# A hybrid decoder step on one core: a sample product over 128 rows, sample states one chunk later, and the last group's square sums read from PSUM and held back

## The chip, the cores and the metric

The kernel runs on one NeuronCore of a Trainium2 chip. The metric is the device time of one execution in microseconds. Five engines work beside each other, each with its own queue that it takes in order: TensorE (PE, matmuls and transposes into the accumulator memory PSUM), VectorE (DVE), ScalarE (ACT), GpSimd (POOL) and SyncE (SP, which issues nearly all DMAs). They wait for each other through semaphores.

## The reference

One layer of a hybrid decoder, run for a prompt of 1024 tokens with 16 learned meta tokens ahead of it, and for 8 samples of 8 tokens each with their own states. Everything is float32. Per layer:

```python
proj = rmsnorm(h, norm_mix_pre) @ w_in            # 1024 -> 4112: gate_b, gate_c, hv, z, xbc, dt
u = gate_c * hv                                   # short convolution mixer
ya = group_rmsnorm(gate_b * causal_dwconv(u, buf_sc, sconv_w), sconv_norm, 8)
xbc = silu(causal_dwconv(xbc, buf_xbc, ssm_conv_w) + ssm_conv_b)
y, s = ssd_chunked(x, softplus(dt + dt_bias), -exp(A_log), B, C, s0, chunk)   # chunks of 128
yb = group_rmsnorm((y + D_skip * x) * silu(z), ssm_norm, 2)
h = h + rmsnorm(concat(ya, yb) @ w_out, norm_mix_post)
fn = rmsnorm(h, norm_ffn_pre)
h = h + rmsnorm((silu(fn @ w_gate) * (fn @ w_up)) @ w_down, norm_ffn_post)
```

Outputs are the layer's result for prompt and samples, and the last states of both convolutions and of the recurrence. Two parts matter here. In `ssd_chunked` a sample's new state is `decay * s0 + sum over its 8 tokens of B_t (dt_t x_t)`, and its output has a term `C_t s0`. And each row of 1024 is normalised twice between the two halves of the layer: once as the out-projection's result, once as the input of the FFN.

## The kernel before

Tokens stand in ten tiles: tile 0 the 16 meta tokens, tiles 1 to 8 the prompt's chunks, tile 9 the 64 sample tokens. Products are made to float32 accuracy by splitting an operand into a rounded high half and the low rest (names in h and l) and running three products: high by high, high by low, low by high.

The program has five stages. Up to about 190 us the inputs are normalised and transposed and the xbc part of the input projection runs (px). From 190 to about 545 us is the mixing stage: for each chunk i the recurrence (`ssd_chunk`: mask tiles M built from the running decay, which is fetched from DRAM as d_a and scaled at L553; products px, po, pd, st), while the remaining parts of the input projection (pz, pc, ph, pb at L220) fill PE in between. Each projected bank in PSUM is freed by a DVE operation: for pz that is L627, for pb L662. The samples' work lies between the chunks: `samples_begin` once, then `sample_state(u)` for the eight states u (a group g of 8 heads, half of the samples, half of the group's heads). A table says after which chunk each is written:

```python
SAMP = {1: (0,), 2: (1,), 3: (2, 3), 4: (4, 5), 5: (6,), 6: (7,)}
```

A state is fetched (s0), transposed on PE into PSUM (s0p, L750), split into three bfloat16 parts (s0t, ACT at L752 and L754, DVE at L753 and L755), and used for the output term (so, L773). The new part is made by PE (s1p, L760 and L761): the samples' x rows stand as high halves in rows 0 to 63 of xs2 and low halves in rows 64 to 127. The first product takes all 128 rows against b1, the high half of B twice; the second takes rows 0 to 63 alone against b2, the low half of B. B is masked per sample into b1 and b2 (bm, L740). DVE scales the old state (L764), adds the new part (L766), and the sum goes to DRAM. s0p, s1p, px and st share two double banks of PSUM (`big`).

From about 528 to 684 us the out-projection runs in three groups of tiles, (1,2,3), (4,9,5), (6,7,8): weights wo are split on ACT (woh, L998) and DVE (wol, L999), and multiplied with the mixed rows' high halves mhb (ACT, L954) and low halves mlb (DVE, L98) into the accumulators o (L1009). Its first group starts while the short convolution's last norms are still made: square (ACT), group sums sn (PE, L668), root (ACT, L669), reciprocal (DVE, L672).

Then the FFN. `residual` takes h = x + rmsnorm(o): a square sum on ACT (ms, L147), the factor on DVE and POOL (mr), and two DVE operations (L899, L900). `fn_tile` makes the FFN's input: square sum (hs), factor (hr), hn (DVE, L916), transposes fT on PE. The FFN's up-projection uses a seven-product scheme of Strassen's kind on blocks of tokens and weights (from 742 to 1163 us; first products from 686); its blocks B01, B11, T1 to T4, B22 are sums of blocks of hn, split at L1191. `first(q)` runs the product whose tokens are ready first: xg and xu over B01, a copy of each accumulator aside (p1g, p1u, ACT at L1079), then on over B11. The copies must be done before PE may go on into the same accumulator. The down-projection follows to the end.

What is written in Python is not the order of the queues: a scheduler walks the program with a simulated timeline and orders each engine's instructions by readiness and by the priorities in `tc.high_priority(offset=...)`. So an edit in one place can reorder the queues far from it.

## Time and profile before

| | |
|---|---|
| Times of three runs | 1406.12, 1403.69, 1406.01 us (median 1406.01) |
| The profiled execution | 1402.11 us, span 1400.4 us |
| TensorE busy | 1369.7 us, 8841 matmul records |
| VectorE busy | 973.9 us |
| ScalarE busy | 586.2 us |
| Sample products over 128 rows (L760) | 16, from 240.9 to 449.8 us |
| Sample products over 64 rows (L761) | 16, from 241.2 to 450.2 us |

A row of a timeline gives start, duration, engine, source line, operation, output and inputs by name, shape and count; in brackets stands the idle time before it and what ended it. Matmul records overlap, so the pace of PE is the distance of starts, not the duration.

### The profile page before, as it was taken

How to read it: one execution, taken by the hardware profiler on the slowest of the kernel's cores; microseconds unless marked ns; L12 is line 12 of the kernel's file. 1: busy time of each engine (PE TensorE's matmuls, PEld its weight loads, DVE VectorE, ACT ScalarE, POOL GpSimd, SP SyncE). 2: the span in 40 equal slices, each digit the busy share in tenths (PEclk: the TensorE clock that was granted, in tenths of full speed). 3: DMA queues.
4: the chain of work that ended last, by engine and by line, in shares of the span. 5: the costliest groups of instructions: out<-in, count | busy, mean ns of one | idle time of the engine just before them, and what ended most of it. 6: DMA issues, size and time to landing. Idle time of an engine off the chain costs nothing.

```text
span 1400.4 us, 22011 instructions
## 1 busy us (share of the span) xinstructions
PE 1369.7 (98%) x8841; PEld 1230.6 (88%) x8841; DVE 973.9 (70%) x1334; ACT 586.2 (42%) x947; POOL 51.8 (4%) x106
## 2 busy tenths in 40 slices
PE   7999999999999999999899999999999999999997
PEld 5889998878888988887799999999999998888886
DVE  6654457868888988767689877666767666455565
ACT  6465345434354354656553232222332334344431
POOL 1000000000000200011100000000000000000001
PEclk9999999999999999999999999999999999999999
DMA  6135346667746457765435553444433479655554
GB/s 214 47 109 148 95 125 198 202 178 205 218 117 208 123 185 256 237 226 196 154 119 167 203 207 113 149 167 168 145 136 103 159 226 341 208 180 165 170 165 139
DMA packets 212543, 240.51 MB, mean 172 GB/s; under 512 B 33421, under 2 KB 161505, under 8 KB 212442
## 3 DMA queue, kind: packets, MB, share of 16 engines
q1 hardware_dynamic: 212442, 239.12, 53.5%
q8 instruction: 69, 1.13, 0.3%
q14 instruction: 32, 0.26, 0.1%
HBM read 170.29 MB, written 68.79 MB: 171 GB/s over the span
## 4 chain that ended last, share of the span: by engine, by line
PE 90%; DVE 3%; DMA 3%; ACT 2%; issue 1%; SPq 1%; POOL 0%; DVEq 0%; POOLq 0%; ACTq 0%
PE d L1393 15%; PE px L220 10%; PE o L1009 9%; PE yu L1050 7%; PE yg L1050 7%; PE pz L220 5%; PE zu L1050 5%; PE zg L1050 5%; PE xg L1050 5%; PE xu L1050 5%; PE pb L220 3%; PE pc L220 3%; PE ph L220 2%; DMA M<-d_a 1%; PE pd L572 1%
## 5 line engine op out<-in xcount | busy, mean ns | idle before, releaser
L220 PE MATMUL px<-xh,whi 128*128 128x272 f32 (+2 forms) x288 | 94.6, 336 | 0.1
L220 PE MATMUL px<-xl,whi 128*128 128x272 f32 (+2 forms) x288 | 93.7, 333 | 0.0
L220 PE MATMUL px<-xh,wlo 128*128 128x272 f32 (+2 forms) x288 | 93.3, 332 | 0.0
L98 DVE TENSOR_TENSOR wlo<-raw,whi 128x1024 fp32r<-128x1024 f32 x32 | 39.0, 1220 | 45.5 <-ACT whi L106 45.4
L999 DVE SCALAR_TENSOR_TENSOR wol<-wo,vec,woh 128x1024 fp32r<-128x1024 f32 x36 | 46.0, 1278 | 32.2 <-ACT woh L998 32.1
L220 PE MATMUL pz<-xh,whi 128*128 128x256 f32 (+2 forms) x192 | 64.6, 337 | 0.0
L220 PE MATMUL pz<-xh,wlo 128*128 128x256 f32 (+2 forms) x192 | 63.9, 333 | 0.0
L220 PE MATMUL pz<-xl,whi 128*128 128x256 f32 (+2 forms) x192 | 63.7, 332 | 0.0
L998 ACT ACTIVATE woh<-wo,vec 128x1024 fp32r<-128x1024 f32 x36 | 41.4, 1149 | 49.1 <-PE o L1009 45.9
L220 PEld LDWEIGHTS px<-xh,whi 128*128 128x128 f32 x288 | 54.4, 192 | 4.6 <-ACT xr L279 0.3
L220 PEld LDWEIGHTS px<-xl,whi 128*128 128x128 f32 x288 | 53.9, 190 | 4.2 <-issue 0.2
L220 PEld LDWEIGHTS px<-xh,wlo 128*128 128x128 f32 x288 | 54.0, 190 | 3.7
L1393 PE MATMUL d<-wd,B01h 128*128 128x512 f32 x176 | 54.2, 389 | 0.0
L252 DVE SCALAR_TENSOR_TENSOR xa<-xr,vec,xa 128x1128 f32<-128x1128 f32 x36 | 50.1, 1391 | 1.2 <-ACT xa L249 0.5
L1393 PE MATMUL d<-wd,T3h 128*128 128x512 f32 x152 | 46.8, 389 | 0.0
L1009 PE MATMUL o<-wol,mhb 128*128 128x512 f32 x144 | 44.4, 394 | 0.2 <-DVE wol L999 0.2
L1393 PE MATMUL d<-wd,B11h 128*128 128x512 f32 x144 | 44.1, 389 | 0.0
L1393 PE MATMUL d<-wd,T2h 128*128 128x512 f32 x144 | 44.1, 389 | 0.0
L279 ACT ACTIVATE xr<-px 128x272 f32<-128x272 f32 (+2 forms) x36 | 16.3, 456 | 60.4 <-PE px L220 60.3
L556 ACT ACTIVATE M<-M,a_tok 128x128 f32<-128x128 f32 (+1 forms) x72 | 21.7, 382 | 46.0 <-DMA M<-d_a 45.1
L1009 PE MATMUL o<-woh,mlb 128*128 128x512 f32 x128 | 40.3, 392 | 0.0
L220 PEld LDWEIGHTS pz<-xh,whi 128*128 128x128 f32 x192 | 36.1, 188 | 3.9 <-issue 1.3
(691 smaller groups left out, 4101.3 us busy)
## 6 DMA issues: line engine op xcount, KB each, us to landing
wo<-in_w_out_dram SPq DMA_DIRECT2D x36, 512.0 KB, 4.8
raw<-in_w_in_dram SPq DMA_DIRECT2D x32, 512.0 KB, 5.3
wg<-in_w_gate_dram SPq DMA_DIRECT2D x11, 1024.0 KB, 8.5
wu<-in_w_up_dram SPq DMA_DIRECT2D x11, 1024.0 KB, 5.3
xr<-in_w_down_dram SPq DMA_DIRECT2D x11, 1024.0 KB, 5.6
d_t<-xr SPq DMA_DIRECT2D x11, 1024.0 KB
xt<-in_x_prompt_dram SPq DMA_DIRECT2D x16, 512.0 KB, 4.8
M<-d_a SPq DMA_DIRECT2D x16, 512.0 KB, 5.4
```

The costliest lines, as they stand in the source:

```text
L98: V.tensor_tensor(out=out, in0=a, in1=hi.bitcast(F32), op=ALU.subtract)
L220: PE.matmul(acc, (hi, lo, hi)[q][:, wk], (xh, xh, xl)[q][t][:, k, o:], start=n_ == 0, stop=n_ + 1 == len(order))
L252: V.scalar_tensor_tensor(out=dst, in0=part(row, i), scalar=wv[:, wcol(i):wcol(i) + 1], in1=dst, op0=ALU.mult, op1=ALU.add)
L279: S.activation(row[:, rc], pt[:, pc], AF.Copy)
L556: S.activation(M[:w, h, :w], M[:w, h, :w], AF.Relu, scale=-1.0, bias=a_s)
L572: PE.matmul(pdv[64 * e:64 * e + 64, h // 2, :w], xd[:w, h * 64:(h + 1) * 64], Ms[h // 8][:w, h % 8, :w], start=True, stop=True)
L998: S.activation(hi, raw, AF.Copy, scale=nv)
L999: V.scalar_tensor_tensor(out=lo, in0=raw, scalar=nv, in1=hi[:, :].bitcast(F32), op0=ALU.mult, op1=ALU.subtract)
L1009: PE.matmul(accs[i][c], l[:, kb, :], r_[:, c * 512:(c + 1) * 512], start=n == 0 and q == 0, stop=n == 11 and q == len(steps) - 1)
L1050: PE.matmul(acc[:, c, 0:W1], w_[l][k], b[r_][:, k, c * W1:(c + 1) * W1], start=start and k == 0 and x == 0, stop=k == 3 and x == 2, skip_g ...
L1393: PE.matmul(accs[t], sx[x][:, tl], wx[y], start=st and x + y == 0, stop=en and x == 1, skip_group_check=n not in OPENS)
```

## The change

Four edits. (1) `SAMP` writes states 3, 5, 6 and 7 one chunk later. (2) The second sample product takes all 128 rows: b2 becomes one buffer of 128 rows, whose lower half is filled with zeros once (a copy of a part of the identity that is off its diagonal) and whose upper half is written as before. (3) In the last group of the out-projection, tiles 6 and 7 are no longer copied to SBUF: their two banks of PSUM lie side by side and are read as one tile by the square sum ms and by the multiplication at L899. Tile 8, whose banks come from elsewhere, is still copied. (4) In `fn_tile` for the last group (in the order 8, 6, 7) a one-column ACT copy from p1g, p1u and p1u is written into the square sum's scratch tile ahead of each square sum, so that the sum can't start ahead of that copy.

```diff
-SAMP = {1: (0,), 2: (1,), 3: (2, 3), 4: (4, 5), 5: (6,), 6: (7,)}
+SAMP = {1: (0,), 2: (1,), 3: (2,), 4: (3, 4), 5: (5,), 6: (6,), 7: (7,)}
...
-    def square_sum(pool, src, w, name):
+    def square_sum(pool, src, w, name, behind=None):
         junk = pool.tile([P, DM], BF16, tag="junk", name=name + "j", bufs=1)
+        if behind is not None:
+            S.activation(junk[:, 0:1], behind[:, 0, 0:1], AF.Copy)
...
+        b2 = po.tile([P, 4, P], F32R, tag="bm2", name="bm2")
+        V.tensor_copy(b2[w:2 * w].rearrange("p a (c n) -> p (a c) n", n=w),
+                      ident[w:2 * w, 0:w].unsqueeze(1).to_broadcast([w, 8, w]))
+        bms["lo"] = b2
...
-            b2 = po.tile([w, 4, P], F32R, tag="bm2", name=f"bm2{u}")
+            b2 = bms["lo"]
...
-            for dst, h in ((b1[0:w], 0), (b1[w:2 * w], 0), (b2, w)):
+            for dst, h in ((b1[0:w], 0), (b1[w:2 * w], 0), (b2[0:w], w)):
...
-            PE.matmul(o, xs2[0:w, xj], b2[:, :, :].rearrange("p b n -> p (b n)"), start=False, stop=True)
+            PE.matmul(o, xs2[:, xj], b2[:, :, :].rearrange("p b n -> p (b n)"), start=False, stop=True)
...
-    def residual(i, h):
+    def residual(i, h, src=None):
...
-        r = rstd_of(square_sum(ph, h[:w, :], w, f"ms{i}"), w, DM, f"mr{i}")
+        src = h if src is None else src
+        r = rstd_of(square_sum(ph, src[:w, :], w, f"ms{i}"), w, DM, f"mr{i}")
...
-        V.scalar_tensor_tensor(out=h[:w], in0=h[:w], scalar=r[:w], in1=post_bc[:w], op0=ALU.mult, op1=ALU.mult)
+        V.scalar_tensor_tensor(out=h[:w], in0=src[:w], scalar=r[:w], in1=post_bc[:w], op0=ALU.mult, op1=ALU.mult)
...
-        r = rstd_of(square_sum(ph, h[:w, :], w, f"hs{i}"), w, DM, f"hr{i}")
+        r = rstd_of(square_sum(ph, h[:w, :], w, f"hs{i}", behind), w, DM, f"hr{i}")
...
-        accs = {i: [bank(f"o{i}{c}") for c in range(2)] for i in tiles}
+        accs, pairs = {}, {}
+        for i in tiles:
+            accs[i] = [bank(f"o{i}{c}") for c in range(2)]
+            if turn[0] % 6 != 2:
+                pairs[i] = turn[1]
...
-        pend = [(i, h_tile(i, accs[i])) for i in tiles]
+        if gi + 1 < len(GROUPS):
+            pend = [(i, h_tile(i, accs[i])) for i in tiles]
+        else:
+            pend = [(i, h_tile(i, accs[i])) if i not in pairs else
+                    (i, ph.tile([P, DM], F32, tag="h", name=f"h{i}", bufs=3), pairs[i]) for i in tiles]
...
-        for args in pend:
-            fn_tile(*args)
+        for args, x in zip(pend, "guu"):
+            fn_tile(*args[:2], p1s[x, 0])
```

The scheduler moves instructions on every engine, most of all in the mixing stage. Three places matter below. Numbers in the names count buffers; line numbers of the changed kernel are higher by 2 in the mixing stage, by 11 in the out-projection and by 7 to 15 in the FFN.

First, ACT where the FFN begins (ms and hs are square sums of tiles 8, 6, 7; h a copy of an accumulator; p1g and p1u the copies that PE waits for). Before:

```order
L147 ACTIVATE ms8j,ms_6447<-h_6433 128x1024
L887 ACTIVATE h_6436<-o_5990 128x512
L979 ACTIVATE weu1hi<-weu_6427 128x1024
L887 ACTIVATE h_6439<-o_5991 128x512
L147 ACTIVATE ms6j,ms_6459<-h_6436 128x1024
L147 ACTIVATE ms7j,ms_6471<-h_6439 128x1024
L147 ACTIVATE hs8j,hs_6591<-h_6433 128x1024
L147 ACTIVATE hs6j,hs_6611<-h_6436 128x1024
L1079 ACTIVATE p1g_6507<-xg_6482 128x544
L147 ACTIVATE hs7j,hs_6631<-h_6439 128x1024
L1079 ACTIVATE p1u_6534<-xu_6509 128x544
```

With the change:

```order
L149 ACTIVATE ms8j,ms_6441<-h_6431 128x1024
L986 ACTIVATE weu1hi<-weu_6425 128x1024
L149 ACTIVATE ms6j,ms_6453<-o_5988 128x1024
L149 ACTIVATE ms7j,ms_6465<-o_5989 128x1024
L1094 ACTIVATE p1g_6501<-xg_6476 128x544
L147 ACTIVATE hs8j<-p1g_6501 128x1
L149 ACTIVATE hs8j,hs_6586<-h_6431 128x1024
L1094 ACTIVATE p1u_6528<-xu_6503 128x544
L147 ACTIVATE hs6j<-p1u_6528 128x1
L149 ACTIVATE hs6j,hs_6607<-h_6434 128x1024
L147 ACTIVATE hs7j<-p1u_6528 128x1
L149 ACTIVATE hs7j,hs_6628<-h_6435 128x1024
```

p1g moved ahead of all three hs, and two copies are gone.

Second, DVE in the mixing stage around the mask scalings of chunk 6 (M_4057 before, M_3995 with the change) and the additions that free the banks of z7 (z_3036 before, z_2980 with the change). Before:

```order
L627 SCALAR_TENSOR_TENSOR z_3036<-z_3036,pz_0_3043 128x256
L518 TENSOR_TENSOR xd_3227<-px_3213,dt 128x1024
L755 TENSOR_TENSOR s0t_2903<-s0p_2894,s0t_2903 128x1024
L779 TENSOR_TENSOR yS<-yS,soe_2887 128x2x32
L518 TENSOR_TENSOR xw_3229<-xd_3227,a_end 128x1024
L543 TENSOR_TENSOR cb_3236<-pcb_3235,U 128x256
L627 SCALAR_TENSOR_TENSOR z_3036<-z_3036,pz_1_3070 128x320
...
L553 TENSOR_SCALAR M_4057<-M_4057,a_tok 128x128 x8
```

With the change:

```order
L770 TENSOR_TENSOR s_3252<-s_3252,ES 128x512
L555 TENSOR_SCALAR M_3995<-M_3995,a_tok 128x128 x8
L770 TENSOR_TENSOR s_3252<-s_3252,ES 128x512
L746 TENSOR_TENSOR bm_3308<-bt_1804,bd_119 64x512 x2
L746 TENSOR_TENSOR bm_1816<-bt_1804,bd_119 64x512
L759 TENSOR_TENSOR s0p_3255<-s0p_3255,s0t_3264 128x1024
L629 SCALAR_TENSOR_TENSOR z_2980<-z_2980,pz_0_2987 128x256
L772 TENSOR_TENSOR s_3252<-s1p_3269,s_3252 128x1024
L629 SCALAR_TENSOR_TENSOR z_2980<-z_2980,pz_1_3014 128x320
```

z7's first two additions moved from ahead of these scalings to behind them, and behind state 3's masks and rescaling.

Third, DVE where the out-projection begins (sq: reciprocals of the last convolution tile; mlb: low halves of tiles 1, 2 and 3; wol: low halves of weights). Before:

```order
L98 TENSOR_TENSOR mlb_5180<-mrb_5177,mhb_5179 128x1024
L98 TENSOR_TENSOR mlb_5186<-mrb_5183,mhb_5185 128x1024
...
L98 TENSOR_TENSOR mlb_5192<-mrb_5189,mhb_5191 128x1024
...
L672 RECIPROCAL sq_5048<-sq_5048 128x128 x2
...
L672 RECIPROCAL sq_5048<-sq_5048 128x160 x2
L999 SCALAR_TENSOR_TENSOR wol_5268<-wo_5265,vec,woh_5267 128x1024
L834 COPY slo<-slp 18x512
L672 RECIPROCAL sq_5048<-sq_5048 128x256 x2
```

With the change:

```order
L674 RECIPROCAL sq_5046<-sq_5046 128x128 x2
...
L98 TENSOR_TENSOR mlb_5178<-mrb_5175,mhb_5177 128x1024
...
L98 TENSOR_TENSOR mlb_5184<-mrb_5181,mhb_5183 128x1024
L1010 SCALAR_TENSOR_TENSOR wol_5224<-wo_5221,vec,woh_5223 128x1024
...
L674 RECIPROCAL sq_5046<-sq_5046 128x160 x2
L840 COPY slo<-slp 18x512
L674 RECIPROCAL sq_5046<-sq_5046 128x256 x2
L675 TENSOR_TENSOR gc_4616<-gc_4616,sq_5046 128x320
L600 RECIPROCAL sg_5293<-sg_5293 128x2x64
L98 TENSOR_TENSOR mlb_5190<-mrb_5187,mhb_5189 128x1024
```

The three mlb moved behind reciprocals that they stood ahead of; the third now stands behind all of them.

More of the change, by code (lines that the diff above doesn't have):

```diff
@@ L701, in hymba_kernel @@
     o_nat = o_s_s[0].rearrange("b g e p n -> b (g e p) n")
+    bms = {}
     def samples_begin():
@@ L723, in samples_begin @@
         return xs2, bt, cs, E, y
-    bms = {}
     def sample_state(u, st):
@@ L910, in hymba_kernel, with fn_tile @@
     psf = []
-    def fn_tile(i, h):
+    def fn_tile(i, h, behind=None):
         t0, w = TT[i]
         xt = ph.tile([P, DM], F32, tag="tok", name=f"hn{i}", bufs=3)
-        r = rstd_of(square_sum(ph, h[:w, :], w, f"hs{i}"), w, DM, f"hr{i}")
+        r = rstd_of(square_sum(ph, h[:w, :], w, f"hs{i}", behind), w, DM, f"hr{i}")
         V.scalar_tensor_tensor(out=xt[:w], in0=h[:w], scalar=r[:w], in1=ffn_bc[:w], op0=ALU.mult, op1=ALU.mult)
```

## The prediction

> **What bounds the kernel now.** I read the page first, then the waits of TensorE, then the granted clock around them, and last the timeline of each engine at the places where the change moves work.
>
> ```profile
> PE 1369.7 (98%) x8841; PEld 1230.6 (88%) x8841; DVE 973.9 (70%) x1334; ACT 586.2 (42%) x947; POOL 51.8 (4%) x106
> PE 90%; DVE 3%; DMA 3%; ACT 2%; issue 1%; SPq 1%; POOL 0%; DVEq 0%; POOLq 0%; ACTq 0%
> ```
>
> TensorE (PE) is busy for 98% of the span and holds 90% of the chain that ends last. So an edit counts only if it takes matmul time away, or makes or fills a gap in PE. The gaps are few. In the view of PE's waits (total us, times, longest):
>
> ```profile
> PE xg L1050 <- ACT p1g L1079: 5.7, 1, 5.7
> PE s0p L750 <- DVE s L766: 2.9, 1, 2.9
> PE yg L1050 <- DVE s2g L1043: 2.6, 1, 2.6
> PE so L773 <- ACT s0t L752: 1.4, 1, 1.4
> ```
>
> Two stand where the FFN begins (xg, yg), two in the mixing stage. A gap can cost more than itself. In the table of stretches (stretch, its length, busy time of PE, its weight loads, DVE, ACT, POOL, then granted clock, DMA share, GB/s) the clock stands in the column after POOL:
>
> ```profile
> 302.30:304.00 1.70, 1.69 (x14) 1.69 (x15) 1.70 (x3) 1.70 (x3) 0.00 (x0) 1.00 0.47 131
> 697.70:699.00 1.30, 1.25 (x5) 1.25 (x6) 0.80 (x3) 1.30 (x3) 0.52 (x1) 0.50 1.05 388
> 699.00:701.00 2.00, 2.00 (x13) 2.00 (x12) 1.93 (x2) 0.25 (x1) 0.58 (x2) 0.59 0.99 277
> 735.00:738.00 3.00, 2.86 (x12) 2.86 (x13) 3.00 (x6) 0.00 (x0) 0.00 (x0) 0.50 0.74 290
> 460.00:545.00 85.00, 85.00 (x544) 72.94 (x543) 79.15 (x91) 36.07 (x60) 9.96 (x5) 1.00 0.54 181
> ```
>
> Behind the 5.7 us gap PE ran 1.3 us at 0.50 and 2 us at 0.59: 0.65 + 0.82, about 1.5 us of work lost. Behind the 2.6 us gap it ran 3 us at 0.50: 1.5 us lost. Behind the 2.9 us gap (s0p, which ends at 302.3) the clock stayed at 1.00. So a gap of this size has cost about 1.5 us more two times in three. The last row is used below: there DVE is busy 79.15 of 85 us, so 5.85 us are free.
>
> **The sample product.** Per state four products run, two over 128 and two over 64 rows, eight states in all. PE's timeline (start, us, engine, line, operation):
>
> ```profile
> 448.92 0.48 PE L760 MATMUL s1p<-bm,xs 128*128 128x512 f32 x1
> 449.33 0.50 PE L761 MATMUL s1p<-bm,xs 64*128 64x512 f32 x1
> ...
> 450.94 0.39 PE L220 MATMUL pb<-xh,whi 128*128 128x512 f32 x1
> 451.18 0.39 PE L220 MATMUL pb<-xh,wlo 128*128 128x512 f32 x1
> 331.14 1.88 PE L608 MATMUL st<-xw,bt 128*128 128x512 f32 x4
> 332.46 0.79 PE L220 MATMUL pz<-xh,whi 128*128 128x512 f32 x1
> ```
>
> From the first sample product to the second pb matmul behind them are 450.94 - 448.92 = 2.02 us for five matmuls (three of the rows left out are two more products and the first pb); two pb matmuls of the same 512 columns follow each other in 0.24. Five at 0.24 would be 1.20, so 0.8 us hang on the alternation of row counts, and 8 x 0.8 = **6.4 us** of PE time if that alone is the cause. The other bound is zero: the st products (331.14) all have 128 rows, yet four of them take 332.46 - 331.14 = 1.32, or 0.33 each. They are the farther row, since they multiply other tiles in another format, while pb shares s1p's stretch; I take 6.4. The Trainium skill has a sentence against it: "TensorE: Matmul & The Clock Gate" (Why this matters for your kernels) says that a matmul over 32 rows takes the same time as one over 128. By that the sum would be 6.4 us higher; the row of 64 at 0.50 beside 0.39 speaks against it, so it is left as a rival.
>
> The low half's zeros are one more DVE copy of 64x512, no dearer than the 0.68 us of the bm row below, in a part where DVE waits on others: nothing.
>
> **States 0 to 2 meet a fixed end.** PE waits at 302.3 for the addition that ends state 2. For this part and the next, from the timeline, the view of DVE's waits and the groups of one tile:
>
> ```profile
> 301.03 1.22 DVE L766 TENSOR_TENSOR s<-s1p,s 128x1024 f32<-128x1024 f32 x1
> DVE M L553 <- DMA M<-d_a: 13.5, 7, 4.6
> 336.41 1.66 DVE L553 TENSOR_SCALAR M<-M,a_tok 128x128 f32<-128x128 f32 x8 [2.12 <-DMA M<-d_a]
> L740 DVE TENSOR_TENSOR bm<-bt,bd x12: 675/685/687, 187.9 to 355.0; 64x512 fp32r<-64x512 f32 x12
> 339.12 0.68 DVE L764 TENSOR_TENSOR s<-s,ES 128x512 f32<-128x512 f32 x1
> 340.85 0.31 PE L220 MATMUL pc<-xl,whi 128*128 128x320 f32 x1
> 341.00 0.31 PE L220 MATMUL pc<-xh,whi 128*128 128x320 f32 x1
> ```
>
> State 3 now goes later, but the px transposes of chunk 4 take the PSUM buffer that s0p of state 3 waited for, and wait for the same addition. So the 2.9 us wait stays. DVE's time there is set by a transfer (the second row, of DVE's waits in the mixing stage: seven waits of its mask work for d_a, the longest 4.6), not by PE; so what states 0 to 2 save, 3 x 0.8 = **2.4 us**, makes that gap longer instead. Left of the 6.4: 4.0.
>
> **State 3 and the masks.** In the new order DVE's eight mask scalings of chunk 6 stand ahead of z7's first addition (the second place shown with the change); before they came after it or well before. z7's third product needs the PSUM bank which that addition frees. Behind the mask's transfer DVE has 1.66 us of scalings, one half of s (0.68), three bm (0.68 each) and the scaling of s0p (1.22 as the first row, which has its size), 5.6 us of rows that overlap by some 0.1 each: 5.2 us. PE has z7's second product to cover it, 24 matmuls at 341.00 - 340.85 = 0.15, or 3.5 us. With the mean wait for d_a, 13.5 / 7 = 1.9, PE waits 1.9 + 5.2 - 3.5 = **3.6 us**. Ends: 0 if DVE arrives early, 4.6 + 5.2 - 3.5 = 6.3. I take the mean.
>
> **States 5, 6 and 7 a chunk later.** Before, one state showed the chain from s0t's copy to its output product (1.4 us, the fourth wait above). One each for two more states that lose their filler: **2.8 us**, ends 0 and 4.2. State 7 brings its DVE work (1.28 rescaling, 1.22 addition, s0p, s0t and two short ones: about 5.5 us) into the stretch 460 to 545 where only 5.85 us are free. PE's products for chunks 7 and 8 wait on that DVE: ends 0 and 5.5; I take **2.0**, as most of that work is ahead of need.
>
> **The start of the out-projection.** The third place shown: before, the low halves mlb3 stood ahead of the last reciprocals, now behind all of them.
>
> ```profile
> 537.05 1.21 DVE L98 TENSOR_TENSOR mlb<-mrb,mhb 128x1024 fp32r<-128x1024 f32 x1
> 540.20 1.02 PE L668 MATMUL sn<-sq,bd 128*128 128x512 f32 x2
> 541.26 0.69 ACT L669 ACTIVATE sq<-sn,eps_c 128x512 f32<-128x512 f32 x1
> 541.97 0.63 PE L1009 MATMUL o<-woh,mlb 128*128 128x512 f32 x2
> 542.44 0.62 PE L1009 MATMUL o<-wol,mhb 128*128 128x512 f32 x2
> 544.09 3.34 DVE L672 RECIPROCAL sq<-sq 128x256 f32<-128x256 f32 x2
> 547.36 0.42 DVE L673 TENSOR_TENSOR gc<-gc,sq 128x320 f32<-128x320 f32 x1
> 548.89 0.94 DVE L598 RECIPROCAL sg<-sg 128x128 f32<-128x128 f32 x1
> ```
>
> From the start of the last sn: 1.02 (sn) + 0.69 (root) + 3.34 + 0.42 + 0.94 + 1.21 = 7.6 less some overlap, 7.5 until mlb3 is there. PE has 541.97 - 540.20 = 1.8 us of sn, slp and the first pair of o, three more pairs at 542.44 - 541.97 = 0.47, and four products of mhb3 at half that: 4.1 us. It waits 7.5 - 4.1 = **3.4 us**, of which the copy mhb3, now behind the roots on ACT, may take the first part. mlb1, mlb2 and two low halves of the weights stand in the same queue: 0.5 each, **2.2** together. Ends of both: 1 (if DVE is a chain ahead) and 8.5.
>
> **The FFN's beginning.** Before, p1g stood on ACT behind hs6's square sum, which waited for an addition of DVE; now it stands ahead of hs8, hs6 and hs7. That wait goes: 5.7 + 1.5 of clock. The rows for the rest, from the timeline:
>
> ```profile
> 689.66 0.69 DVE L888 COPY h<-o 128x512 f32<-128x512 f32 x1
> 691.65 0.41 PE L1050 MATMUL xu<-B01h,weul 128*128 128x272 f32 x2
> 694.73 2.35 DVE L900 TENSOR_TENSOR h<-h,xt 128x1024 f32<-128x1024 f32 x2
> 694.96 1.39 POOL L141 TENSOR_TENSOR hr8r<-hr,mhalf 128x1 f32<-128x1 f32 x1 [2.21 <-DVE hr L139]
> 697.00 1.28 DVE L916 SCALAR_TENSOR_TENSOR hn<-h,hr8r,ffn_bc 128x1024 f32<-128x1024 f32 x1
> 729.73 2.42 DVE L1191 TENSOR_TENSOR T1l<-xr,T1h 128x2176 fp32r<-128x2176 f32 x1
> 732.07 2.42 DVE L1191 TENSOR_TENSOR B22l<-xr,B22h 128x2176 fp32r<-128x2176 f32 x1
> ```
>
> The multiplications of s2g now come ahead of the low halves T1l and B22l on DVE: 2.6 + 1.5 go. In all 11.3. What is late next is hn8: on DVE its factor still stands behind both additions of h6 and h7 (694.73). Without the two copies for h6 and h7 (0.69 each) these end near 695.7 instead of 697.1; hr8r takes up to 1.39, half of it at least, and hn8 1.28: 697.7 to 698.4. PE ends its xu at 691.9 (two matmuls in 0.25), goes on with 24 matmuls of xg and 8 of xu at 0.125, 4.0 us, and asks for hn8 at 695.9. New wait 1.8 to 2.5, 1.9 taken since PE's matmuls may start a little late too, and 0.4 for hn7 behind it. B22l and T1l, 4.8 us of DVE, are pushed to the products that read them: 0 to 4.8, 3.0 taken. Net -11.3 + 5.3 = **-6.0**; ends -9.5 (1.8 and nothing else) and -3.6 (2.5 + 0.4 + 4.8).
>
> **Sum.** -6.4 + 2.4 + 3.6 + 2.8 + 2.0 + 3.4 + 2.2 - 6.0 = +4.0, and 1.5 for one of the two gaps of some 3.5 us (z7, mlb3) that the clock answers: **+5.5**. The profiled execution took 1402.1 and would take 1407.6. It lies 3.9 under the median of the runs shown, 1406.0, from which I forecast **1411.5**. The Trainium skill ("TensorE: Matmul & The Clock Gate", What's actually happening) puts the drop of the clock behind an idle window of about 3.4 us; the trace disagrees in that a 2.6 us gap was enough. By that page the clock's 1.5 might fall away, and the time would be 1410.
>
> **Rivals.** One on the other side: *the waits are covered*. It is one mechanism, the transfer of d_a for chunk 6: landing before DVE's scalings are due, it leaves DVE a chain ahead, and z7, the later states and mlb3 keep their cover. It decides once the transfer lands 3.6 us earlier, against PE, than at the mean. For it: such waits have a mean of 1.9 and reach 4.6, so they scatter by about that much, and DVE has 5.85 us free behind. Against: 93% of DVE is taken at the place. Then -4.0 - 6.0 + 3 for what remains = 1399. Second, *gains and waits cancel*: half of the mixing and out-projection terms (7 of 14): 1406 - 10 + 7 = 1403, with the clock's share up to 1408. Third, *full price*: all upper ends, 6.3 + 4.2 + 5.5 + 8.5 + 3 of clock - 10 = +17: up to 1423. Fourth, *the 128 rows save nothing*, since what holds a sample product is its tile's weight load as with st: +4.0 on the forecast, 1415.5. That the change does not hold p1g ahead is excluded by the order of ACT.
>
> **Chances.** A measurement here can tell about 0.2%, 2.8 us. Covered (below 1403.2) 0.18; cancel (to 1408.8) 0.20; the forecast (1408.8 to 1416) 0.42; full price 0.13; no saving 0.07. Slower 0.62, same 0.20, faster 0.18. The range 1401 to 1419 leaves out the better half of the first case (0.10) and the dearer half of the third (0.07). The forecast's own range is 1408.8 to 1416.
>
> **What would show it.** Right: sample products 0.23 apart; PE's wait for p1g gone, a wait of 1.8 to 2.5 of fT for hn; PE waits of 3 us or more at px for s, at pz for z, and at o for mlb. Wrong: sample products still 0.4 apart; no wait over 1 us between 520 and 560; PE idle in the mixing stage no more than before; or the half clock gone at the FFN with nothing new in its place, which would put the time under 1403.

## The result, and the profile after

The changed kernel takes 1415.46 us (median of 6 runs, 1411.8 to 1417.88) against 1406.07 (6 runs, 1403.69 to 1409.21) for the kernel before, measured beside it: a ratio of 1.0065, with a 95% interval of 1.0044 to 1.0085. It is slower by 9.4 us, where 5.5 were forecast. The profiled execution shows the same: its span is 1410.1 us, against 1400.4. From the page of the changed kernel (span, busy time by engine, the chain that ended last):

```profile
span 1410.1 us, 22007 instructions
PE 1369.6 (97%) x8841; PEld 1232.6 (87%) x8841; DVE 974.0 (69%) x1333; ACT 585.3 (42%) x948; POOL 51.7 (4%) x106
PE 79%; DVE 10%; DMA 6%; ACT 3%; issue 2%; SPq 0%; POOL 0%; DVEq 0%; POOLq 0%; ACTq 0%
```

PE is busy for as long as before (1369.6 against 1369.7 us), although its sample products became cheaper, and the span grew by 9.7. PE's share of the last chain fell from 90% to 79%, and DVE (3% to 10%) and DMA (3% to 6%) took it. (The chain follows one releaser at each step; PE itself is still busy for 97% of the span.) So PE now waits more often, and what it gained on the products was spent on something else. The view of PE's waits (total us, times, longest) names the new gaps:

```profile
PE pz L222 <- DVE z L629: 4.0, 2, 3.8
PE o L1020 <- ACT mhb L961: 4.0, 2, 3.7
PE px L507 <- DVE s L772: 2.8, 1, 2.8
PE so L779 <- ACT s0t L758: 2.6, 3, 1.6
PE fT L935 <- DVE hr L139: 2.1, 1, 2.1
PE so L779 <- ACT s0t L760: 1.1, 1, 1.1
```

The waits of 5.7 us for p1g and 2.6 us for s2g at the beginning of the FFN have shrunk to 0.7 and 0.4, and one of 1.5 us for u3g is new. Three waits of 2.8 to 3.8 us stand in the mixing stage and at the start of the out-projection. The clock answered all three, and also the 2.1 us wait of fT. In the table of stretches (length, busy PE, weight loads, DVE, ACT, POOL, then granted clock, DMA share, GB/s), the 8 us behind each of these four waits:

```profile
300.00:308.00 8.00, 8.00 (x50) 7.80 (x51) 7.01 (x8) 3.77 (x6) 0.24 (x1) 0.79 0.90 261
330.80:338.80 8.00, 8.00 (x33) 6.55 (x34) 3.08 (x4) 1.46 (x3) 0.00 (x0) 0.79 0.45 131
552.60:560.60 8.00, 7.95 (x28) 6.37 (x29) 6.08 (x10) 3.84 (x5) 0.00 (x0) 0.79 0.71 204
712.10:720.10 8.00, 8.00 (x55) 8.00 (x55) 5.07 (x5) 3.36 (x6) 1.10 (x2) 0.79 0.23 70
```

The work lost in a stretch is its length times what is missing from a clock of 1.00: 8 x 0.21, 1.7 us each. A busy PE at a lower clock counts as busy, which is why its busy time did not fall.

**Where the 9.7 us come from.** I compared the two traces by the starts of PE's matmuls between two points that both have: the first pz matmul (187.3 us before, 186.3 after) and the first product of the out-projection's second operand (569.5 before, 583.4 after). This stretch became 14.9 us longer:

| part of PE's time in it | us |
|---|---|
| idle, 5.3 before, 18.9 after | +13.6 |
| sample products (32 steps, 13.0 before, 7.6 after) | -5.4 |
| the products that follow them (pb, pc) | -0.8 |
| other matmuls (pz +2.8, o +2.4, norms sn and pn +1.1, px and ph +0.6 each) | +7.5 |

Of the last row 5.0 us are the three drops of the clock (3 x 1.68); 2.5 are spread over rows that I could not put down to one cause. The FFN then gave back 4.2 us (the start of xg lies 13.9 us later, the end 9.7).

**The sample product** did what it was to do. In the view of one tile (durations in ns, least, median, most; first and last start), before and after:

```profile
L760 PE MATMUL s1p<-bm,xs x16: 391/488/502, 240.9 to 449.8; 128*128 128x512 f32 x16
L761 PE MATMUL s1p<-bm,xs x16: 492/498/502, 241.2 to 450.2; 64*128 64x512 f32 x16
```
```profile
L766 PE MATMUL s1p<-bm,xs x16: 389/393/478, 239.9 to 493.6; 128*128 128x512 f32 x16
L767 PE MATMUL s1p<-bm,xs x16: 388/394/397, 240.1 to 493.8; 128*128 128x512 f32 x16
```

**z7 and state 3.** DVE's timeline in the changed kernel (start, us, engine, line, operation; in brackets the idle time before it and what ended it), and PE's matmul that waits for it:

```profile
324.88 1.66 DVE L555 TENSOR_SCALAR M<-M,a_tok 128x128 f32<-128x128 f32 x8 [2.32 <-DMA M<-d_a]
326.45 0.69 DVE L770 TENSOR_TENSOR s<-s,ES 128x512 f32<-128x512 f32 x1
327.05 2.10 DVE L746 TENSOR_TENSOR bm<-bt,bd 64x512 fp32r<-64x512 f32 x3
329.18 1.23 DVE L759 TENSOR_TENSOR s0p<-s0p,s0t 128x1024 f32<-128x1024 f32 x1
330.32 0.41 DVE L629 SCALAR_TENSOR_TENSOR z<-z,pz 128x256 f32<-128x256 f32 x1
```
```profile
330.79 0.61 PE L222 MATMUL pz<-xh,whi 128*128 128x512 f32 x1 [3.81 <-DVE z L629]
```

DVE waits 2.32 us for d_a, works through masks, rescaling, bm and s0p, and begins the addition that frees the bank 5.4 us after the transfer came; the bank is free after 5.9 us. PE waits 3.81 us.

**The start of the out-projection.** The timelines of SP (queue times, not transfers), ACT, PE and DVE in the changed kernel:

```profile
533.43 2.42 SPq L954 DMA_DIRECT2D mrb<-d_yb  x2
542.31 2.06 SPq L954 DMA_DIRECT2D mrb<-d_yb  x2
```
```profile
551.54 2.25 ACT L961 ACTIVATE mhb<-mrb 128x1024 fp32r<-128x1024 f32 x2 [2.23 <-DMA mrb<-d_yb]
552.65 1.03 PE L1020 MATMUL o<-woh,mhb 128*128 128x512 f32 x2 [3.74 <-ACT mhb L961]
```
```profile
541.05 1.23 DVE L98 TENSOR_TENSOR mlb<-mrb,mhb 128x1024 fp32r<-128x1024 f32 x1 [0.67 <-ACT mhb L961]
548.35 3.33 DVE L674 RECIPROCAL sq<-sq 128x256 f32<-128x256 f32 x2
552.82 1.15 DVE L98 TENSOR_TENSOR mlb<-mrb,mhb 128x1024 fp32r<-128x1024 f32 x1
```

PE stops for 3.74 us, but not for mlb3, as forecast: it stops for mhb3, ACT's copy of a transfer that landed near 551.5. The transfer was issued only at 542.3, since mrb has two buffers and the first is free when mlb1 (541.05 to 542.28) has read it. mlb3, the forecast wall, ends at 553.97, about when PE comes to it.

Why mlb1 itself is late stands on SP's queue. The first two transfers of mrb went out at 533.43 and 535.35, some 16 us later than before, while PE's first product of the out-projection starts when it did (541.1 us, 541.4 before). SP takes its queue in order, and ahead of them stands the transfer of the samples' output rows (yS), which the program issues after state 7. SP's wait for it in the changed kernel (to 520.58 us), and SP's row of the first two transfers in the kernel before:

```profile
SPq L787 <- DVE yS L785: 9.9, 1, 9.9
```
```profile
517.64 1.61 SPq L947 DMA_DIRECT2D mrb<-d_yb  x2
```

Before, the rows of yS had gone out at 474.06.

### The profile page after: what moved, and what is told of

It is laid out like the page before. It is cut to its first block, busy times and chain, and to the rows that moved or that the text cites. A ratio compares the mean times of both kernels' runs of the same rounds, so it can differ in the third digit from the quotient of the medians.

```text
span 1410.1 us, 22007 instructions
## 1 busy us (share of the span) xinstructions
PE 1369.6 (97%) x8841; PEld 1232.6 (87%) x8841; DVE 974.0 (69%) x1333; ACT 585.3 (42%) x948; POOL 51.7 (4%) x106
## 4 chain that ended last, share of the span: by engine, by line
PE 79%; DVE 10%; DMA 6%; ACT 3%; issue 2%; SPq 0%; POOL 0%; DVEq 0%; POOLq 0%; ACTq 0%
PE d L1408 15%; PE px L222 10%; PE o L1020 8%; PE yg L1065 7%; PE yu L1065 7%; PE zg L1065 4%; PE zu L1065 4%; PE xu L1065 4%; PE pz L222 4%; PE xg L1065 4%; PE pc L222 3%; DMA M<-d_a 3%; PE pb L222 1%; PE d5s L1419 1%; PE d1s L1419 1%
## 5 line engine op out<-in xcount | busy, mean ns | idle before, releaser
L1020 PE MATMUL o<-woh,mhb 128*128 128x512 f32 x144 | 40.6, 404 | 4.8 <-ACT mhb L961 4.0
```

Source lines behind the costliest of these rows:

```text
L1020: PE.matmul(accs[i][c], l[:, kb, :], r_[:, c * 512:(c + 1) * 512], start=n == 0 and q == 0, stop=n == 11 and q == len(steps) - 1)
```

## The experiments

In each diff "before" or "after" names the kernel that the edit is made to. Each run was timed beside the kernel before, whose median lay between 1405.5 and 1407.7.

| | us (median) | ratio to before | 95% interval |
|---|---|---|---|
| the whole change | 1415.46 | 1.0065 | 1.0044 to 1.0085 |
| 1 the table alone | 1421.14 | 1.0108 | 1.0093 to 1.0123 |
| 2 the product alone | 1404.83 | 0.9993 | 0.998 to 1.0005 |
| 3 the two FFN edits alone | 1401.97 | 0.9968 | 0.9956 to 0.9979 |
| 4 all but the table | 1399.7 | 0.9954 | 0.994 to 0.9968 |
| 5 state 3 a chunk later alone | 1420.55 | 1.009 | 1.0073 to 1.0106 |
| 6 states 5, 6, 7 a chunk later alone | 1415.22 | 1.0044 | 1.0026 to 1.0062 |
| 7 state 7 a chunk later alone | 1403.08 | 0.9971 | 0.9954 to 0.9989 |
| 9 the hold of the square sums alone | 1403.2 | 0.9978 | 0.9966 to 0.9991 |
| 10 square sums from PSUM alone | 1405.82 | 1.0 | 0.9989 to 1.0012 |
| 11 the whole change, another table | 1398.05 | 0.9941 | 0.9926 to 0.9957 |
| 12 the whole change, mrb on another queue | 1416.86 | 1.0073 | 1.0055 to 1.009 |

(8 is a measurement of gaps, not a part of the change.)

### 1 to 4: the parts alone

Run 1, the table alone (to before):

```diff
-SAMP = {1: (0,), 2: (1,), 3: (2, 3), 4: (4, 5), 5: (6,), 6: (7,)}
+SAMP = {1: (0,), 2: (1,), 3: (2,), 4: (3, 4), 5: (5,), 6: (6,), 7: (7,)}
```

> Only the table of states is changed (3, 5, 6 and 7 a chunk later); products and FFN as before. Theory A (the table reorders the queues, and its waits with the half clock behind them are the whole loss): the three long PE waits (px for s, pz for z at 3 to 4 us, o for mhb or mlb at 3 to 4 us) are there, with the half clock behind them; idle time between 190 and 585 us about 18 us against 5; time 1418 to 1425 us. Rival B (the loss comes from the single b2 buffer, whose masks must wait for the last product): at most one of these waits, time 1405 to 1409 us.

It costs 1.08%, some 15 us. From its view of PE's waits:

```profile
PE o L1009 <- ACT mhb L954: 3.5, 3, 3.0
PE px L505 <- DVE s L766: 3.3, 1, 3.3
PE pz L220 <- DVE z L627: 3.1, 1, 3.1
```

All three places of the forecast are there without any other edit, so the table makes them.

Run 2, the product alone (to before):

```diff
-            b2 = po.tile([w, 4, P], F32R, tag="bm2", name=f"bm2{u}")
+            b2 = bms["lo"]
...
-            PE.matmul(o, xs2[0:w, xj], b2[:, :, :].rearrange("p b n -> p (b n)"), start=False, stop=True)
+            PE.matmul(o, xs2[:, xj], b2[:, :, :].rearrange("p b n -> p (b n)"), start=False, stop=True)
```

> Only the second sample product over 128 rows with the zero half; table and FFN as before. Theory A: sample products 0.23 us apart, 6 us of PE time less, of which up to 2.4 us go into the wait of s0p for state 2 (2.9 us before); time 1400 to 1404 us, no new wait over 1.5 us. Rival B: new waits of the masks bm for the product or of PE for the masks, time 1406 us or more.

The steps of its 32 sample products sum to 7.57 us against 13.03, a gain of 5.5; yet the time is that of the kernel before within what can be told. The mixing stage in the table of stretches, first of the kernel before and then of run 2, and run 2's waits there:

```profile
240.00:545.00 305.00, 299.73 (x2044) 255.73 (x2043) 256.47 (x345) 133.98 (x245) 14.10 (x12) 1.00 0.63 186
```
```profile
240.00:545.00 305.00, 294.20 (x2037) 255.82 (x2036) 253.85 (x343) 136.19 (x250) 13.27 (x12) 0.99 0.62 183
PE s0p L754 <- DVE s L770: 3.9, 1, 3.9
PE so L777 <- ACT s0t L756: 2.9, 3, 1.4
```

PE is busy 5.53 us less in the same 305 us: all of it became idle time. The wait at 302 grew by 1.0, the so waits by 1.5 (1.4 before), and small ones for z, gc and px (0.5 to 1.0 each) took the rest. On top came one drop of the clock behind the longer wait, 1.7 us, where the profile of the kernel before had none. I had let 2.4 be absorbed; in this profile everything was. The scheduler also placed the queues anew for this edit, so how much of it is absorption and how much new order is not told apart.

Run 3, both FFN edits without the table and the product (to after: the old table and the old b2 put back).

> Only the two FFN edits (PSUM read directly, square sums held behind the copies); table and product as before. Theory A: the waits for p1g (5.7 us) and s2g (2.6 us) and the half clock behind them are gone, hn8 is waited for (1.5 to 2.2 us) and about 2 us of later waits remain: 4 to 6 us less, 1400 to 1402 us. Rival C (the waits only move and the gain in the changed kernel is an accident of its order): within 1.5 us of before.

It gains 0.32%, about 4.3 us. PE waits 2.08 us for hn8 at fT, 0.64 for hn7 and 0.71 and 1.47 at the products behind.

Run 4, the whole change with the old table:

```diff
-SAMP = {1: (0,), 2: (1,), 3: (2,), 4: (3, 4), 5: (5,), 6: (6,), 7: (7,)}
+SAMP = {1: (0,), 2: (1,), 3: (2, 3), 4: (4, 5), 5: (6,), 6: (7,)}
```

> The whole change with the old table. Theory A: the gains of product and FFN add up, 8 to 11 us less than before: 1395 to 1398 us, and none of the waits at pz for z or o for mhb over 1.5 us. Rival B: 1404 us or more, since the new product brings the waits with it.

The gain is 6.6 us, less than the 8 to 11 expected: beside the FFN edits the product is worth 2.3 us by the medians (1401.97 to 1399.7), not 4 or more, and as the intervals of runs 3 and 4 overlap, even that is not clear of noise. Run 1 and run 4 together (+14.9 and -6.6) give +8.3 for the change; 9.4 was measured.

### 5 to 7: which state costs what

Each is an edit of the table of before:

```diff
 run 5
-SAMP = {1: (0,), 2: (1,), 3: (2, 3), 4: (4, 5), 5: (6,), 6: (7,)}
+SAMP = {1: (0,), 2: (1,), 3: (2,), 4: (3, 4, 5), 5: (6,), 6: (7,)}
 run 6
+SAMP = {1: (0,), 2: (1,), 3: (2, 3), 4: (4,), 5: (5,), 6: (6,), 7: (7,)}
 run 7
+SAMP = {1: (0,), 2: (1,), 3: (2, 3), 4: (4, 5), 5: (6,), 7: (7,)}
```

> The kernel before with one entry of the table changed: state 3 goes from behind chunk 3 to behind chunk 4 (3: (2,), 4: (3, 4, 5)). Theory A (each late state makes its own wait: state 3 that of pz for z, the later ones that of o): the wait at pz for z, 3 to 4 us, is there with px's wait for s, and no wait of o for mhb or mlb over 1.9 us; time 1409 to 1415 us. Rival D (the waits belong to the whole order and come from any move alike): also a wait of o for mhb or mlb of 2.5 us or more, or no wait at pz over 2 us.

> The kernel before with the other entries changed: states 5, 6 and 7 a chunk later, state 3 as before (3: (2, 3), 4: (4,), 5: (5,), 6: (6,), 7: (7,)). Theory A: no wait of pz for z over 2 us at 330; a wait of o for mhb or mlb of 2.5 to 4 us near 550, with the half clock behind it; time 1410 to 1418 us. Rival D: the wait at pz is there too, or none at o.

> The kernel before with state 7 alone a chunk later (6: none, 7: (7,)). Theory A1 (it is state 7's 5.5 us of DVE work between 460 and 545 us, where DVE has 5.85 us free, that makes the out-projection wait): o waits for mhb or mlb 2.5 us or more; time 1409 to 1413 us. Rival A2 (states 5 and 6 do it, by the chain of the norms behind them; state 7 alone leaves the low halves ahead of the reciprocals): waits of o under 1.6 us, small waits of 0.5 to 1 us elsewhere; time 1405 to 1409 us.

Run 5 has the wait at z7; run 6 has none there, and has two at the start of the out-projection. From PE's timelines of run 5, then run 6:

```profile
301.00 1.09 PE L505 MATMUL px<-ident,xb 128*128 128x128 f32 x8 [2.04 <-DVE s L766]
332.50 0.57 PE L220 MATMUL pz<-xh,whi 128*128 128x512 f32 x1 [3.78 <-DVE z L627]
```
```profile
540.42 0.73 PE L1009 MATMUL o<-woh,mhb 128*128 128x512 f32 x2 [2.06 <-ACT mhb L954]
550.21 1.22 PE L1009 MATMUL o<-woh,mhb 128*128 128x512 f32 x2 [2.49 <-ACT mhb L954]
```

So state 3 makes the z7 stall, and states 5, 6 and 7 make the one at the out-projection. The size of run 5 was missed: state 3 alone costs 0.9%, more than was expected, since with three states behind chunk 4 PE also waits for pb's bank twice (3.8 us in all) and the clock drops more often.

Run 7 separates two reasons for the out-projection's stall. If state 7's own DVE work, placed where DVE has 5.85 us free, were the cause, this run would show the stall. It shows one wait of 0.54 us at the first o, and the kernel is 0.29% faster than before. That reason falls: the stall needs state 5 or 6, or both, late as well. The time lies below the expected 1405 to 1409. The gain itself comes from elsewhere: the wait for p1g fell to 1.3 us, as the scheduler had placed the FFN's queues otherwise. An edit 200 us upstream had moved them.

### 8: how long a gap the clock answers

Twelve waits were put into the down-projection of before, where PE otherwise never stops: a group of products is closed, ACT makes one to eight long copies and then reads the accumulators, and PE can go on into them only after that.

```diff
+    gj = pd.tile([P, 256], BF16, name="gj", bufs=1)
+    gap_at = {(n, q): 1 + (2 * m + o) % 8 for m, n in enumerate(ORDER) for o, q in ((0, 2), (3, 5)) if n != 1}
...
+                if (n, q) in gap_at:
+                    for _ in range(gap_at[n, q]):
+                        S.activation(gj, accs[3][:, 0:256], AF.Copy)
+                    for t in range(4):
+                        S.activation(gj[:, 0:8], accs[t][:, 0:8], AF.Copy)
```

> The kernel before, with twelve waits put into the down-projection: ahead of 12 blocks of products PE must wait until ACT has read all four accumulators; 1 to 8 further short copies stand ahead of these reads, so the waits last some 1 to 4.5 us. The numbers computed are the same. Theory H (a wait of about 2 us or more can drop the granted clock to one half for some 3.4 us, by chance of its position): waits under 1.5 us keep the clock at 1.00; of those over 2 us more than half are followed by 3 to 3.5 us at 0.50; each such costs 1.5 to 1.8 us beside the wait. Rival T (a fixed limit near 3.4 us): every wait above it and none below drops the clock.

One run took 1453.51 us; nine of the twelve gaps came out over 1 us. Two of them on PE's timeline:

```profile
1349.40 0.73 PE L1395 MATMUL d<-wd,B11h 128*128 128x512 f32 x2 [2.20 <-ACT gj L1420]
1389.20 0.92 PE L1395 MATMUL d<-wd,B01h 128*128 128x512 f32 x2 [1.90 <-ACT gj L1420]
```

and the stretches of 3.41 us around them (the clock is the third number from the end; why these stretches is told below):

```profile
1345.20:1348.61 3.41, 2.00 (x9) 1.31 (x7) 1.92 (x2) 2.80 (x6) 0.00 (x0) 1.00 0.16 40
1348.61:1352.03 3.42, 2.63 (x12) 2.17 (x12) 0.00 (x0) 1.03 (x5) 0.00 (x0) 1.00 0.80 272
1386.16:1389.57 3.41, 1.51 (x8) 0.93 (x7) 1.23 (x1) 3.06 (x11) 0.00 (x0) 1.00 0.45 154
1389.57:1392.98 3.41, 3.41 (x10) 2.67 (x9) 0.00 (x0) 0.00 (x0) 0.00 (x0) 0.50 0.00 0
```

The gap of 1.90 dropped the clock and the one of 2.20 did not. I then took the gaps of PE behind 100 us in the profiles of all fourteen kernels of this study, the clock in the 8 us behind each:

| gap, us | gaps | answered by a drop |
|---|---|---|
| 1.0 to 1.5 | 30 | 1 |
| 1.59 to 1.9 | 8 | 3 |
| 2.04 to 2.31 | 10 | 4 |
| 2.49 to 3.52 | 21 | 18 |
| 3.63 to 7.14 | 16 | 16 |

The three of the fourth row that were not answered have 2.87, 2.91 and 3.34 us. An answer costs 1.4 to 1.8 us in most cases, and 2.7 to 3.1 in seven, all behind gaps of 3.3 us or more. So the clock has no fixed limit at 3.4 us of gap here: by its length alone a gap has a chance, which rises from next to nothing at 1.5 us to certainty at 3.6. The losses gather at 8 x 0.21 = 1.68 us, which is a clock of a half for 3.4 us. The Trainium skill ("TensorE: Matmul & The Clock Gate", What's actually happening) has an idle window of about 3.4 us as the condition; below that length these runs disagree with it.

What decides a gap's case is where it lies. The traces keep the start and end of every drop: in each of the fourteen profiles all drops begin whole multiples of 3.413 us apart, to within 0.01 us. So the clock is set anew at the ends of pieces of that length. I cut the profiles into these pieces, from 100 us to about 10 us before PE's last matmul, 5277 in all, and took PE's idle time in each:

| piece | PE idle in it, us | pieces | next piece at 0.50 |
|---|---|---|---|
| at full clock | 0 to 1.86 | 5186 | 1 |
| at full clock | 1.87 to 3.41 | 41 | 41 |
| at 0.50 | 0 to 0.59 | 42 | 0 |
| at 0.50 | 0.62 to 3.13 | 8 | 8 |

The one exception (1.23 us idle, run 5, at 388 us) is not explained. Above, the gap of 1.90 lay in one piece; the one of 2.20 was cut into 1.41 and 0.79. A gap over 3.74 us, twice 1.87, can't be cut so that both parts stay below, and a drop goes on for a second piece when that piece holds 0.62 us or more of idle time. This rule was read from the traces afterwards, and no run was made to test it.

### 9 and 10: the two FFN edits apart

Run 9, the hold alone, and run 10, the square sums from PSUM alone (to before; of run 9 and of run 10 the core):

```diff
 run 9
+        if behind is not None:
+            S.activation(junk[:, 0:1], behind[:, 0, 0:1], AF.Copy)
...
-        for args in pend:
-            fn_tile(*args)
+        for args, x in zip(pend, "guu"):
+            fn_tile(*args[:2], p1s[x, 0])
 run 10
-        r = rstd_of(square_sum(ph, h[:w, :], w, f"ms{i}"), w, DM, f"mr{i}")
+        src = h if src is None else src
+        r = rstd_of(square_sum(ph, src[:w, :], w, f"ms{i}"), w, DM, f"mr{i}")
```

> The kernel before with the square sums held behind the copies, and nothing else: tiles 6 and 7 are still copied to SBUF. Theory A (holding alone takes away the wait for p1g; reading PSUM directly only brings hn8 earlier by the two copies on DVE, 1.4 us): no wait for p1g over 1 us, fT waits for hn8 about 3.5 us (2.1 with both edits), the wait for s2g gone; time 1401 to 1404 us. Rival E (the copies' removal is what counts): within 1.5 us of before.

> The kernel before with tiles 6 and 7 read straight from PSUM, and nothing else; nothing holds the square sums. In its order all three hs stand ahead of p1g, and PE's transposes of tile 8 ahead of xg over B11. Theory A: the wait only changes its name, fT for hn8 of 5 to 6.5 us near 692 with the half clock behind it, no wait for p1g; time 1404 to 1407 us. Rival E: a wait under 3 us and 1402 us or less.

The hold alone gains 0.22% (2.3 us): the waits for p1g and s2g are replaced by 2.98 us of fT, with a drop of the clock behind it. The PSUM reads alone gain nothing; the wait only takes another name:

```profile
699.57 1.08 PE L929 MATMUL fT<-ident,hn 128*128 128x128 f32 x4 [7.14 <-DVE hr L139]
```

Without the hold PE now waits 7.1 us for hn8 (more than was expected) instead of 5.7 for p1g. Together they gain more by the medians (4.3 us) than the sum of both alone (2.3 + 0), though the intervals of runs 3 and 9 overlap. The likely reason: the hold puts the copies first, and the PSUM reads shorten the chain to hn8 that is late next (fT waits 2.08 us in run 3 against 2.98 in run 9).

### 11: the same change with another table

```diff
-SAMP = {1: (0,), 2: (1,), 3: (2,), 4: (3, 4), 5: (5,), 6: (6,), 7: (7,)}
+SAMP = {1: (0, 1), 2: (2,), 3: (3,), 4: (4, 5), 5: (6,), 6: (7,)}
```

> The whole change with a table that goes the other way: states 1, 2 and 3 a chunk earlier than in the old table (1: (0, 1), 2: (2,), 3: (3,), 4: (4, 5), 5: (6,), 6: (7,)). Theory A (what the table costs or gives is whether a state's chain ends under filler or in front of PE): the wait of 3 us for state 2 near 300 and its half clock go, 4.5 us in all, and waits of so or s0p for other states of 1 to 2.5 us come in their place; time 1394 to 1400 us, against 1399.7 with the old table. Rival F (earlier is safe, since filler is left behind it): no new wait over 1 us, 1393 to 1395 us.

States 1, 2 and 3 come earlier than before, or as early, instead of later. This is the fastest version measured: 0.59% under the kernel before, 1.2% under the changed one, and 1.7 us under run 4, with which its range overlaps. In the table of stretches PE is full at all three places:

```profile
296.00:306.00 10.00, 10.00 (x70) 7.69 (x69) 7.86 (x10) 0.44 (x1) 0.68 (x1) 1.00 0.93 230
326.00:336.00 10.00, 10.00 (x84) 8.06 (x80) 7.08 (x16) 3.83 (x10) 0.00 (x0) 1.00 1.12 268
540.00:556.00 16.00, 16.00 (x73) 13.26 (x72) 11.83 (x15) 5.34 (x6) 0.00 (x0) 1.00 0.80 259
```

What is left are waits of 2.3 us at 339 (no drop of the clock) and a few near 1 us.

### 12: the late transfer on a queue of its own

By then the stall at mhb3 was read as a transfer late in SP's queue. Here the second and third transfer of mrb go out on POOL's queue; the order on PE, DVE and ACT is that of the changed kernel.

```diff
-            SY.dma_start(raw[:, :, :w], src)
+            (G if part == "b" and i in (2, 3) else SY).dma_start(raw[:, :, :w], src)
```

> Base: the changed kernel. The second and third transfer of mixed rows (mrb, 128x1024, for the first group of the out-projection) are issued by POOL on its own queue instead of SP's; the order of DVE, ACT and PE is word for word that of the changed kernel. There PE waited 3.74 us at the first o products of tile 3 for ACT's copy mhb, which waited for the transfer issued at 542.3 behind four others and landed near 551.5. Theory T (the transfer alone made the stall): mhb3 is done before 548, the wait at o falls below 1 us together with its half clock, and the time falls by 4 to 5.5 us to 1410 to 1412. Theory D (DVE's chain is a second wall of nearly the same length: reciprocals to 551.7 and 552.9, then mlb3 until 553.97): the wait for mhb goes, PE asks for mlb3 about 1 us of products later, near 550, and waits 3.3 to 4 us for it, under the name of mlb, with the half clock behind it; the time stays within 2 us of the changed kernel's, 1413 to 1417.

Neither theory's picture came. The time is that of the changed kernel (1416.86), but the wait is still one for mhb. From run 12's timelines of POOL, ACT and PE, and its list of transfers (KB each, us from issue to landing):

```profile
543.71 0.54 POOL L954 DMA_DIRECT2D mrb<-d_yb  x1 [32.04 <-DVE mlb L98]
551.97 2.01 ACT L961 ACTIVATE mhb<-mrb 128x1024 fp32r<-128x1024 f32 x2 [1.80 <-DMA mrb<-d_yb]
553.08 1.22 PE L1020 MATMUL o<-woh,mhb 128*128 128x512 f32 x2 [3.32 <-ACT mhb L961]
mrb<-d_yb POOLq DMA_DIRECT2D x1, 512.0 KB, 8.2
```

The run did not put its question. The third transfer was issued at 543.71, no earlier than in the changed kernel (542.31), because it waits for mlb1, and mlb1 for the first transfer, which this edit leaves on SP's queue: it went out at 533.90, behind yS as in the changed kernel. The second, on POOL's queue, went out at 510.95 instead of 535.35, so its place in SP's queue is what had held that one back. Once issued, the third took 8.2 us on a queue of its own, too; in the kernel before it took at most 3.8 (issued at 526.93, copied by ACT from 530.74). The stretches in which it is fetched, in the changed kernel and in the kernel before (DMA share and GB/s at the end of the row):

```profile
536.00:552.00 16.00, 12.55 (x53) 8.87 (x51) 15.30 (x19) 7.45 (x11) 0.00 (x0) 1.00 0.99 359
```
```profile
526.90:534.70 7.80, 7.80 (x40) 6.68 (x39) 7.80 (x8) 4.17 (x6) 0.00 (x0) 1.00 0.40 139
526.93 7.73 SPq L947 DMA_DIRECT2D mrb<-d_yb  x3
```

Before, the third transfer went out at 526.93 (the x3 are the third and the next group's first two) with the DMA engines 40% busy, ahead of the norm weights and the prompt rows (post_bc, ffn_bc, xt). With the change it goes out 15 us later and runs beside them, at a DMA share of 0.99. That DVE's chain would stop PE next, at mlb3, if the transfer came early, was not put to the test, since the transfer did not come earlier. To move the first transfer, or the one of yS, to another queue would put the question; neither was tried, nor a third buffer for mrb.

## Why the prediction was right and wrong

The sign and the places were right, the sum was 4 us short, and the measured time lies in the range and in the forecast's own case. Step by step:

- **Sample product, -6.4.** Measured -5.4 on its own steps and -0.8 on the products behind. The step between starts is 0.24 us, as the row of pb had it. The rival that 128 rows save nothing falls. So does, for this sequence, the reading of the Trainium skill ("TensorE: Matmul & The Clock Gate", Why this matters for your kernels) by which the row count makes no difference: alternating 128 and 64 rows cost 0.17 us more per matmul.
- **States 0 to 2 meet a fixed end, +2.4.** The wait at 302 was to grow from 2.9 to 5.3 and stayed at 2.8 in the changed kernel. In run 2 it grew by 1.0 and other waits took the rest. Run 2 shows that a gain on PE can become idle time as a whole; where it would be absorbed was wrong.
- **z7, +3.6.** Measured 3.81, with the chain as forecast (wait for d_a 2.32 against the mean of 1.9 taken). Run 5 shows that state 3 makes it. The best-sized term of the sum, in part by luck: beside the longer wait, DVE's chain to the free bank took 5.9 us instead of 5.2, and PE had 4.4 us of work left when DVE began to wait, instead of 3.5; 2.3 + 5.9 - 4.4 is near 1.9 + 5.2 - 3.5.
- **so, +2.8, and state 7, +2.0.** The so waits are 3.7 in all against 1.4 before: +2.3. For chunks 7 and 8 waits of 1.0 (pd), 1.0 (sn) and 0.8 (pc) were measured, 2.8; the cause named for them, state 7's DVE work alone, was not confirmed: run 7, which moves only that state, shows 0.54 at the first o and 0.6 at pb and is faster than before.
- **Start of the out-projection, +5.6.** Measured 3.74 + 0.26 + 0.49 = 4.5. The place was right and the releaser wrong: not the reciprocals ahead of mlb3, but a transfer that was issued late because mlb1 freed its buffer late. I costed the row order of DVE and missed that a late reader of a two-buffer tile also delays the next fetch, into a time when the DMA engines are full; and I left out the order of SP's queue, where state 7's rows (yS) now hold up the first fetch by some 16 us. That the fetch is what ends the wait, and that SP stands 9.9 us for yS ahead of it, is shown by the traces. The four kernels with this stall (changed, 1, 6 and 12) all have that wait of 9.9, and their first fetch goes out 7 to 8 us ahead of the first product; in runs 5 and 7, which lack the stall, it goes out 11 to 13 us ahead. That earlier issue would cure it is only argued.
- **FFN, -6.0.** Measured -4.2 on PE; the two edits alone gain 4.3 (run 3). The waits did what was forecast and a little more: they fell from 8.5 to 4.7 us (fT 2.1, u3g 1.5, p1g 0.7, s2g 0.4), by 3.8 where 3.0 were forecast. The 3.0 of the clock did not come: matmul time fell by 0.4. fT's wait of 2.1 lies in the forecast 1.8 to 2.5, but I gave it no drop of the clock, and it had one (1.7 us).
- **The clock, +1.5.** This is the term that was mis-sized. All three waits of the mixing stage and the out-projection were answered: 3 x 1.7 = 5.0 us, against 1.5. I had counted two gaps at one chance in two, and the px wait at none since its clock had stayed at 1.00 before. By the table of pieces z7 (3.81) had to be answered and the wait for mhb (3.74) all but had to, and px was a matter of place: its 2.79 us lay within one piece, while the 2.87 of before had been cut so that no piece held more than 1.85 us of idle time. In the stretch up to the out-projection the idle time was 2.8 us smaller than forecast (13.6 against 2.4 + 3.6 + 2.8 + 2.0 + 5.6 = 16.4), other matmuls 6.0 dearer (7.5 against 1.5), the product 0.2 worse: 3.4 in all. Add 1.8 from the FFN and take off the 1.0 that this execution was ahead at 186 us (the profile of before had lost 1.7 to a drop of the clock at 62 us, this one had not; that is luck), and it is the 4.2 by which the span's 9.7 exceeds 5.5.

Of the rivals, *the waits are covered* falls: DVE waited 2.32 us for d_a and was late. *Gains and waits cancel* describes run 2, not the whole. *Full price* had the clock nearer, at 3 us, and still too low.

## What to carry to other kernels

When PE is at 98% and a queue's order is set by a scheduler, price an edit of the order by the gaps it opens, and give every gap over 2.5 us the clock's 1.7 us as well (18 of 21 were answered up to 3.5 us, 16 of 16 above); a gap kept at its old length is not safe either, since its place in the clock's pieces moves. A gain on the busiest engine counts only up to the next point whose end another engine or a transfer sets: here 5.5 us of faster matmuls alone gave no measurable gain. For a tile with few buffers, follow its late reader on to the next fetch, and look at what the DMA engines will be doing by then. Compare the order of the queue that issues the transfers too: one transfer that waits for late data holds up all that stand behind it.

## What the runs showed of the hardware that was not expected

- The half clock follows gaps of the same length sometimes and sometimes not: 1.90 us yes and 2.20 us no in one execution; 2.79 yes in the changed kernel and 2.91 no in run 12, at the same place, with the same order of work around it. What decides is the idle time within one piece of 3.413 us: 41 of 41 pieces with 1.87 us or more were followed by one at 0.50, 1 of 5186 with less. Run 12's 2.91 us were cut into pieces with 1.2 and 1.7 us of idle time.
- Matmuls over 128 and 64 rows in turn step by 0.41 us (13.03 us for 32) and over 128 rows alone by 0.24 (7.60 for 32), with the same columns.
- With the DMA engines at a share of 0.95 to 1.0, 512 KB took 8.2 us from issue to landing on a queue that held nothing else ahead of it; at a share of 0.40 it took at most 3.8.
